# A streaming-encoder step: narrower gathered rows, a 112-sum top-k and gates from expert 68

## The chip, the cores and the metric

The kernel runs on one core of a Trainium2 chip. The metric is the device time of one execution in microseconds (us), lower is better. The engines are called as in the profile: PE (TensorE matmul), PEld (its weight loads), DVE (VectorE), ACT (ScalarE), POOL (GpSimd) and SP (SyncE, here only an issuer of DMAs).

## The reference, cut to what matters

One layer of an encoder over 288 tokens (256 of a prompt, 32 of a running stream), width 2048, in float32. First comes an attention mixer with an output projection and a layer norm, and then a mixer in which each token chooses among 16384 single-neuron experts. Only the second one is touched:

```python
q = (xt @ w_q).reshape(T, 8, 2, 128)
s = einsum('thcd,hcnd->thcn', q, sub_keys)              # 8 heads, 2 halves, 128 keys
sv, si = top_k(s, 16)
cand = sv[:, :, 0, :, None] + sv[:, :, 1, None, :]       # 16 x 16 sums per head
best, pos = top_k(cand, 16)
experts = si[.., pos // 16] * 128 + si[.., pos % 16]     # written with take_along_axis
gates = softmax(best)
out = sum over the 128 chosen experts of gelu(x . u[e]) * gate * v[e]
```

`sv` comes sorted from the largest down, so of the 256 sums of a head only those can be among the best 16 that have few enough sums above and to the left of them.

## The kernel before, in words

The work has five stages, one after the other on the PE: the projections and the attention; the output projection; the query projection of the experts (16 tiles, `proj(rh, rl, NQ)`); the **U stage**, which multiplies all 128 x 128 experts' u-rows with 224 of the tokens; and the **V stage**, which multiplies the gated activations with the v-rows. Every weight is split by ACT into a high part (L164) and by DVE into a rest (L180), and the PE multiplies both; in the U stage an expert block, called an expert from here on, takes 16 pairs of products (L976, L978).

The tokens are dealt with in three groups, `ROWS = (128, 96, 128)`: groups 0 and 1 are the 224 dense tokens. The last 64 tokens, the **gathered** ones (group 2), don't go through U and V: their u- and v-rows are fetched by indirect DMAs from POOL (`Rows.fetch`, L885) and multiplied on DVE (`use_u` L900, `use_v` L1063). Each of the 64 tokens stands twice, on partitions 0 to 63 with four heads and on 64 to 127 with the other four. So their normalised rows `x1g` are wanted on all 128 partitions.

`residual(c, ps)` (L605) runs once for each of the 16 column tiles of the output projection. It adds the residual, and on the PE it transposes two groups of 128 tokens (L614) and lays the 64 gathered tokens twice with two matmuls against the identity, one to each half of the partitions (L616). DVE then takes statistics (L619), and ACT copies the gathered part into `x1g` (L620). `norm_job` (L765) turns the statistics into mean and scale, and `rows_job` (L753) normalises `x1g` in two halves of 1024 columns (L757, L759, L761).

The work beside the products is interleaved by hand. `tick()` (L210) is called four times in each expert (after products 3 and 7 of each of its halves). A tick advances every generator in `stages` by a step, and then spends a budget on the queue `slow`: each tick adds `pace["rate"]` to it, and each `yield` of a generator in `slow` names the cost that is taken from it. The rate is 0.4 in the query stage (L861), 0.62 at the start of the U stage (L967), and `URATE = 0.38` from the moment that the gathered tokens' choice is known (L1015). In `slow` stand, in this order of completion: `rows_job`; `topk` for the pieces (0: heads 0, 4), (2: pairs 0-1), (2: pairs 2-3); `gathered_choice` (L741), which sets the flag for the rate; three more `topk` of group 0; `dense_choice(0)`; four `topk` of group 1; `dense_choice(1)`. A `topk` (L645) works on two heads at once: it finds the best 16 of 128 keys twice, forms the 256 sums (L677), finds the best 16 of them (L684 to L695), and recovers the two key numbers by a comparison with `iota`, a product and a sum (L702 to L709). A `dense_choice` (L727) makes the softmax on ACT and DVE, transposes the two key numbers and the gate on the PE (L733), copies them (L735) and negates the gate (L738).

From expert `G0` on, the gates of the dense tokens are made: one-hot matrices on DVE and ACT (`one_hots`, L903 to L912), two tokens for each half of an expert, four small matmuls on the PE (L956), and a product or copy into the activations (`gate_in`, L915). They take 112 halves, with four more for the pipeline. All of `slow` has to be done by then, so in expert `G0 - 1`, after its first half, the kernel empties the queue there and then, in program order:

```python
if i == G0 - 1 and half == 0:        # L996
    while slow:
        drain(slow.popleft())
...
if i < G0:                           # L1016
    ug.upto(GFIRST * (n + 1 - g_from) // (2 * G0 - g_from))
else:
    ug.upto(GFIRST + (128 - GFIRST) * (n + 1 - 2 * G0) // (2 * (NKEY - G0) - 4))
```

`ug.upto` paces the 128 gathered u-rows: `GFIRST = 40` of them before expert `G0`, and 88 after it. The order of the DMAs is that of POOL's program for the indirect ones and of SP's for the weights (L190).

Of the kernel before, what the change touches and what calls it, by code (L numbers as in the profile page):

```python
# [9 lines left out]
F32 = mybir.dt.float32  # L10
# [3 lines left out]
AF = mybir.ActivationFunctionType  # L14
OP = mybir.AluOpType
AX = mybir.AxisListType

P = 128
D = 2048
DT = 16  # L20
NTOK = 288
NQ = NTOK + 2
ND = 224
# [11 lines left out]
K = 16  # L35
# [5 lines left out]
KT = [0, 1, 2, 3, 4, 5, 6, 7, 8, 9, 12, 13, 14, 15, 10, 11]  # L41
AHEAD = 2
RAW = 4
G0 = 64
GFIRST = 40
VEND = 230
URATE = 0.38
# [3 lines left out]
def tile_stream_step(ctx: ExitStack, tc, xT_d, memT_d, ckT_d, cv_d, cmkT_d, cmv_d,  # L51
# [3 lines left out]
    nc = tc.nc  # L55
    const = ctx.enter_context(tc.tile_pool(name="const", bufs=1))
# [24 lines left out]
    x1g = keep.tile([P, D], F32, tag="x1g", name="x1g")  # L81
# [64 lines left out]
    at = {"load": 0, "split": 0, "take": 0}  # L146
# [108 lines left out]
    def rsqrt(pool, out, v, n, rows=P):  # L255
# [14 lines left out]
    ident = const.tile([P, P], F32, tag="ident", name="ident")  # L270
# [4 lines left out]
    iota = const.tile([P, NKEY], F32, tag="iota", name="iota")  # L275
    nc.gpsimd.iota(iota, pattern=[[1, NKEY]], base=0, channel_multiplier=0,
                   allow_small_or_imprecise_dtypes=True)
    lncol = const.tile([P, 2, DT], F32, tag="lncol", name="lncol")
    nc.gpsimd.dma_start(lncol, lncol_d)
    hot = memp.tile([32, NREL], F32, tag="hot", name="hot")  # L280
# [29 lines left out]
    for u in range(8):  # L310
        hi, lo = take()
# [282 lines left out]
    grow = nat.tile([P, 2, D], F32, tag="grow", name="grow")  # L594
    stat = nat.tile([P, 3, DT, 6], F32, tag="stat", name="stat")
    mvr = nat.tile([P, 3, 4], F32, tag="mvr", name="mvr")
    for c in range(0, DT, 4):
        nc.gpsimd.dma_start(rT[:, c:c + 4], xT_d[:, c:c + 4])

# [5 lines left out]
    def residual(c, ps):  # L605

        r, g = rT[:, c], lncol[:, 0, c:c + 1]
        nc.vector.scalar_tensor_tensor(r, r, ALPHA, ps[:, :NTOK], op0=OP.mult, op1=OP.add)
        nc.scalar.activation(rh[:, c, :NTOK], r, AF.Copy, scale=g)
        yield  # L610
        nc.vector.scalar_tensor_tensor(rl[:, c, :NTOK], r, g, rh[:, c, :NTOK].bitcast(F32), op0=OP.mult, op1=OP.subtract)
        tp = pb()
        for t in range(2):
            nc.tensor.transpose(tp[:, t * P:(t + 1) * P], r[:, t * P:(t + 1) * P], ident)  # L614
        for t in range(2):
            nc.tensor.matmul(tp[64 * t:64 * t + 64, 2 * P:3 * P], r[:, ND:NTOK], ident, start=True, stop=True)  # L616
        yield
        for t in range(3):
            nc.vector.bn_stats(stat[:, t, c], tp[:, t * P:(t + 1) * P])  # L619
        nc.scalar.copy(x1g[:, c * P:(c + 1) * P], tp[:, 2 * P:3 * P])  # L620

    def start_residual(c, ps):
        g = residual(c, ps)
# [21 lines left out]
    def topk(units):  # L645


        V = nc.vector
        n, t, R = len(units), units[0][0], ROWS[units[0][0]]
        key = f"{t}_{units[0][1]}"  # L650
        step = units[-1][1] - units[0][1] or 1
        hs = slice(units[0][1], units[-1][1] + 1, step)

        def new(tag, shape, dt=F32):
            return tw.tile([P, 2] + shape, dt, tag=tag, name=f"{tag}{key}")[:R, :n]
        S = [s_all[:R, u] for *_, u in units]
        sv, si, sf = new("sv", [2, K]), new("si", [2, K], U32), new("sf", [2, K])
        s2, ca, pos = new("s2", [2, NKEY]), new("ca", [K, K]), new("pos", [K], U32)
        ab, abf = new("ab", [2, K], U32), new("abf", [2, K])
        bv = best[:R, t, hs]  # L660
        both = [(q, c) for c in range(2) for q in range(n)]
        for q, c in both:
            V.max(out=sv[:, q, c, 0:8], in_=S[q][:, c])
        for q, c in both:
            V.max_index(out=si[:, q, c, 0:8], in_max=sv[:, q, c, 0:8], in_values=S[q][:, c])
            if c == 0 and q == n - 1:
                yield 0.64 * n
        yield 0.22 * n
        for q, c in both:
            V.match_replace(out=s2[:, q, c], in_to_replace=sv[:, q, c, 0:8], in_values=S[q][:, c], imm_value=-3.0e38)  # L670
        yield 0.43 * n
        for q, c in both:
            V.max(out=sv[:, q, c, 8:16], in_=s2[:, q, c])
        yield 0.43 * n
        for q, c in both:
            V.max_index(out=si[:, q, c, 8:16], in_max=sv[:, q, c, 8:16], in_values=s2[:, q, c])
        V.tensor_tensor(out=ca, in0=sv[:, :, 0].unsqueeze(3).to_broadcast([R, n, K, K]),  # L677
                        in1=sv[:, :, 1].unsqueeze(2).to_broadcast([R, n, K, K]), op=OP.add)
        yield 0.7 * n
        V.tensor_copy(sf.rearrange("p q c k -> p (q c k)"), si.rearrange("p q c k -> p (q c k)"))  # L680
        cf = [ca[:, q].rearrange("p a b -> p (a b)") for q in range(n)]
        c2 = [s2[:, q].rearrange("p a b -> p (a b)") for q in range(n)]
        for q in range(n):
            V.max(out=bv[:, q, 0:8], in_=cf[q])  # L684
        yield 0.4 * n
        for q in range(n):
            V.match_replace(out=c2[q], in_to_replace=bv[:, q, 0:8], in_values=cf[q], imm_value=-3.0e38)
        for q in range(n):
            V.max_index(out=pos[:, q, 0:8], in_max=bv[:, q, 0:8], in_values=cf[q])
        yield 0.7 * n  # L690
        for q in range(n):
            V.max(out=bv[:, q, 8:16], in_=c2[q])
        yield 0.35 * n
        for q in range(n):
            V.max_index(out=pos[:, q, 8:16], in_max=bv[:, q, 8:16], in_values=c2[q])  # L695
        V.tensor_scalar(ab[:, :, 0], pos, 4, None, op0=OP.logical_shift_right)
        V.tensor_scalar(ab[:, :, 1], pos, 15, None, op0=OP.bitwise_and)
        V.tensor_copy(abf.rearrange("p q c k -> p (q c k)"), ab.rearrange("p q c k -> p (q c k)"))
        yield 0.5 * n
        eq = (ca, s2.rearrange("p q c (a b) -> p q (c a) b", b=K))  # L700
        for c in range(2):
            V.tensor_tensor(out=eq[c], in0=iota[:R, 0:K].unsqueeze(1).unsqueeze(1).to_broadcast([R, n, K, K]),  # L702
                            in1=abf[:, :, c].unsqueeze(3).to_broadcast([R, n, K, K]), op=OP.is_equal)
        yield 0.62 * n
        for c in range(2):
            V.tensor_tensor(out=eq[c], in0=eq[c], in1=sf[:, :, c].unsqueeze(2).to_broadcast([R, n, K, K]), op=OP.mult)
        yield 0.62 * n
        for c, en in ((0, e1n), (1, e2n)):
            V.tensor_reduce(out=en[:R, t, hs], in_=eq[c], op=OP.add, axis=AX.X)  # L709
        yield 0.62 * n  # L710
# [41 lines left out]

    def rows_job():  # L753

        for a in range(2):
            cs = slice(a * 1024, (a + 1) * 1024)
            nc.scalar.activation(x1g[:, cs], x1g[:, cs], AF.Identity, bias=mvr[:, 2, 3:4], scale=mvr[:, 2, 2:3])  # L757
            yield 0.6
            nc.vector.tensor_mul(x1g[:, cs], x1g[:, cs], grow[:, 0, cs])  # L759
            yield 1.15  # L760
            nc.vector.tensor_add(x1g[:, cs], x1g[:, cs], grow[:, 1, cs])  # L761
            yield 1.15
        ns.close()

    def norm_job():  # L765

        yield
        for t in range(3):
            nc.vector.bn_aggr(mvr[:, t, 0:2], stat[:, t].rearrange("p a b -> p (a b)"))
        rsqrt(nat, mvr[:, :, 2], mvr[:, :, 1], 3)  # L770
        nc.vector.scalar_tensor_tensor(mvr[:, :, 3], mvr[:, :, 0], -1.0, mvr[:, :, 2], op0=OP.mult, op1=OP.mult)
        nc.vector.tensor_scalar(mvr[:, :, 0], mvr[:, :, 0], -1.0, None, op0=OP.mult)
        wide = nat.tile([P, 3, 2, P], F32, tag="wide", name="wide")
        for j in range(2):
            nc.vector.tensor_copy(wide[:, :, j], mvr[:, :, 2 * j:2 * j + 1].to_broadcast([P, 3, P]))
        yield
        yield
        yield
        tp = [pb(), pb()]
        for j in range(2):  # L780
            for t in range(2):
                nc.tensor.matmul(tp[j][:, t * P:(t + 1) * P], wide[:, t, j], ident, start=True, stop=True)
            nc.tensor.matmul(tp[j][:, 2 * P:NTOK], wide[32:64, 2, j], ident[32:64, 32:64], start=True, stop=True)
        yield
        for j in range(2):
            nc.scalar.copy(across[:, j], tp[j][:, :NTOK])
        flags["norm"] = True
        slow.append(rows_job())
        yield
        for d in range(DT):  # L790
            stages.append(normed(d))
            for _ in range(3 + d % 2):
                yield
# [174 lines left out]
    for i in range(NKEY):  # L968
        ps = pa()
        for half in range(2):  # L970
            n = 2 * i + half
            hi, lo = take()
# [8 lines left out]
            if n == 1:  # L981
# [5 lines left out]
                for h in range(0, 8, 2):  # L987
# [6 lines left out]
                                                                                 name="bigA")  # L994
# [348 lines left out]
```

## Time and profile before

| | |
|---|---|
| median of 3 runs | 2029.88 us (2026.51 to 2029.91) |
| the profiled execution | 2030.04 us, its span 2028.3 us |
| PE busy | 1988.4 us, 98% of the span |
| DVE busy | 1583.5 us, 78% |
| ACT busy | 1160.4 us, 57% |
| POOL busy | 496.7 us, 24% |

The span runs from the first to the last instruction, and the time holds some 1.7 us around it. A busy engine is one with an instruction under way. Matmuls overlap, so the duration of one is no measure of what it costs the PE; the distance between the starts of two is.

### The profile page before, as it was taken

How to read it: one execution, taken by the hardware profiler on the slowest of the kernel's cores; microseconds unless marked ns; L12 is line 12 of the kernel's file. 1: busy time of each engine (PE TensorE's matmuls, PEld its weight loads, DVE VectorE, ACT ScalarE, POOL GpSimd, SP SyncE). 2: the span in 40 equal slices, each digit the busy share in tenths (PEclk: the TensorE clock that was granted, in tenths of full speed). 3: DMA queues.
4: the chain of work that ended last, by engine and by line, in shares of the span. 5: the costliest groups of instructions: out<-in, count | busy, mean ns of one | idle time of the engine just before them, and what ended most of it. 6: DMA issues, size and time to landing. Idle time of an engine off the chain costs nothing.

```text
span 2028.3 us, 34887 instructions
## 1 busy us (share of the span) xinstructions
PE 1988.4 (98%) x13156; PEld 1871.1 (92%) x13156; DVE 1583.5 (78%) x2646; ACT 1160.4 (57%) x1916; POOL 496.7 (24%) x360
## 2 busy tenths in 40 slices
PE   9999999999999999998899999999999999999996
PEld 7999999999999999997899999999999999999996
DVE  5455555565789898899899999978888888888886
ACT  5445545533555555554799999954444445444453
POOL 0100000010000212122233333333444443343412
PEclk8999999999999999999899999999999999999998
DMA  7854455475456788887688888888999998999985
GB/s 269 267 165 149 147 158 150 128 250 148 147 155 187 265 280 278 275 276 258 216 295 296 296 294 302 295 305 302 335 328 340 327 328 318 327 324 328 324 264 170
DMA packets 145770, 520.43 MB, mean 257 GB/s; under 512 B 16785, under 2 KB 18977, under 8 KB 145473
## 3 DMA queue, kind: packets, MB, share of 16 engines
q1 hardware_dynamic: 101200, 358.66, 54.2%
q0 software_dynamic: 44400, 159.53, 21.5%
q8 instruction: 104, 1.70, 0.3%
q14 instruction: 66, 0.53, 0.1%
HBM read 507.54 MB, written 10.06 MB: 255 GB/s over the span
## 4 chain that ended last, share of the span: by engine, by line
PE 91%; DVE 5%; ACT 2%; DMA 1%; issue 1%; POOL 0%; SPq 0%; POOLq 0%; DVEq 0%; ACTq 0%
PE pa L976 21%; PE pa L1152 11%; PE pb L1152 11%; PE pa L978 10%; PE pa L231 7%; PE pa L232 6%; PE pa L233 6%; PE pb L1154 5%; PE pa L1154 5%; PE pb L956 2%; DVE lo L180 2%; ACT hi L164 1%; PE pa L931 1%; DMA raw<-in_wmv 1%; PE pb L396 0%
## 5 line engine op out<-in xcount | busy, mean ns | idle before, releaser
L180 DVE TENSOR_TENSOR lo<-raw,hi 128x1024 fp32r<-128x1024 f32 (+1 forms) x680 | 821.6, 1210 | 338.6 <-ACT hi L164 326.2
L164 ACT CAST hi<-raw 128x1024 fp32r<-128x1024 f32 (+1 forms) x680 | 705.8, 1039 | 448.0 <-PE pa L1152 277.2
L976 PE MATMUL pa<-ux,hi 128*128 128x448 f32 x2048 | 671.7, 379 | 0.0
L978 PE MATMUL pa<-ux,lo 128*128 128x224 f32 x2048 | 544.3, 266 | 0.9 <-DVE lo L180 0.9
L976 PEld LDWEIGHTS pa<-ux,hi 128*128 128x128 f32 x2048 | 386.4, 189 | 29.8 <-issue 0.2
L978 PEld LDWEIGHTS pa<-ux,lo 128*128 128x128 f32 x2048 | 392.4, 192 | 1.4 <-DVE lo L180 1.4
L1152 PE MATMUL pa<-hs,hi 128*128 128x448 f32 x1020 | 338.2, 376 | 0.0
L1152 PE MATMUL pb<-hs,hi 128*128 128x448 f32 x1020 | 337.9, 375 | 0.0
L885 POOL DMA_INDIRECT ur<-in_u,gidx x128 | 204.4, 1597 | 513.5 <-DVE ur L900 351.9
L885 POOL DMA_INDIRECT vr<-in_v,gidx x128 | 225.9, 1765 | 350.3 <-DVE x1g L1063 320.3
L1154 PE MATMUL pb<-hs,lo 128*128 128x224 f32 x1020 | 271.0, 266 | 0.3 <-DVE lo L180 0.3
L1154 PE MATMUL pa<-hs,lo 128*128 128x224 f32 x1020 | 270.9, 266 | 0.0
L1152 PEld LDWEIGHTS pb<-hs,hi 128*128 128x128 f32 x1020 | 191.4, 188 | 17.5
L1152 PEld LDWEIGHTS pa<-hs,hi 128*128 128x128 f32 x1020 | 191.4, 188 | 17.4
L1154 PEld LDWEIGHTS pb<-hs,lo 128*128 128x128 f32 x1020 | 194.8, 191 | 0.5 <-DVE lo L180 0.5
L231 PE MATMUL pa<-xh,hi 128*128 128x288 f32 x640 | 195.1, 305 | 0.0
L1154 PEld LDWEIGHTS pa<-hs,lo 128*128 128x128 f32 x1020 | 194.8, 191 | 0.0
L232 PE MATMUL pa<-xl,hi 128*128 128x288 f32 x640 | 188.8, 295 | 0.0
L233 PE MATMUL pa<-xh,lo 128*128 128x288 f32 x640 | 188.1, 294 | 0.0
L1063 DVE SCALAR_TENSOR_TENSOR x1g<-vr,ggate,x1g 128x1024 f32<-128x1024 f32 x128 | 163.6, 1278 | 0.0
L900 DVE SCALAR_TENSOR_TENSOR ur<-ur,x1g 128x1024 f32<-128x1024 f32 x128 | 155.7, 1216 | 2.3 <-DMA ur<-in_u,gidx 2.3
L231 PEld LDWEIGHTS pa<-xh,hi 128*128 128x128 f32 x640 | 120.0, 187 | 4.9 <-issue 3.7
(341 smaller groups left out, 2721.0 us busy)
## 6 DMA issues: line engine op xcount, KB each, us to landing
raw<-in_ut SPq DMA_DIRECT2D x256, 512.0 KB
raw<-in_v SPq DMA_DIRECT2D x255, 512.0 KB
raw<-in_win SPq DMA_DIRECT2D x80, 512.0 KB
raw<-in_wq SPq DMA_DIRECT2D x32, 512.0 KB
raw<-in_wo SPq DMA_DIRECT2D x29, 512.0 KB
raw<-in_wmv SPq DMA_DIRECT2D x8, 512.0 KB
raw<-in_wmk SPq DMA_DIRECT2D x6, 512.0 KB
rT<-in_xT POOLq DMA_DIRECT2D x4, 576.0 KB
```

Source lines behind the costliest of these rows:

```text
L164: nc.scalar.copy(hi[:, cs], raw[:, cs])
L180: nc.vector.tensor_sub(lo, raw, hi.bitcast(F32))
L231: nc.tensor.matmul(ps[:, :n], wh, mh[:, d, :n], start=(d == 0), stop=False)
L232: nc.tensor.matmul(ps[:, :n], wh, ml[:, d, :n], start=False, stop=False)
L233: nc.tensor.matmul(ps[:, :n], wl, mh[:, d, :n], start=False, stop=(d == DT - 1))
L885: nc.gpsimd.indirect_dma_start(out=t, out_offset=None, in_=self.table, in_offset=bass.IndirectOffsetOnAxis(ap=gidx[:, a, s:s + 1], axis=0))
L900: nc.vector.scalar_tensor_tensor(rows, rows, 1.0, x1g[:, a * 1024:(a + 1) * 1024], op0=OP.mult, op1=OP.mult, accum_out=gact[:, a, s:s + 1])
L976: nc.tensor.matmul(ps[:, :2 * ND], wh, ux[:, d].rearrange("p a t -> p (a t)"), start=(d == 0), stop=False, skip_group_check=True)
L978: nc.tensor.matmul(ps[:, :ND], wl, ux[:, d, 0], start=False, stop=False, skip_group_check=True)
L1063: nc.vector.scalar_tensor_tensor(va, rows, ggate[:, s:s + 1], va, op0=OP.mult, op1=OP.add)
L1152: nc.tensor.matmul(accs[dt][:, :2 * ND], wh, hb.rearrange("p a t -> p (a t)"), start=(i == 0), stop=False, skip_group_check=True)
L1154: nc.tensor.matmul(accs[dt][:, :ND], wl, hb[:, 0], start=False, stop=False, skip_group_check=True)
```

## The change

It has three parts. In `residual` one transpose lays the 64 gathered tokens on partitions 0 to 63 alone; the statistics, the copy and `rows_job` work on 64 partitions; and `rows_job` copies each half of the finished `x1g` to partitions 64 to 127 by a DMA from POOL. In `topk` the sums are 112 for each head, rows 0 to 3 of the first list with all 16 of the second, and rows 4 to 15 with the first 4 of the second; the position is turned back into two key numbers by comparisons with a new constant `first`; and the costs named at the `yield`s are lower. And `G0` is 68.

```diff
-G0 = 64
+G0 = 68
...
+    first = const.tile([P, 2, K], F32, tag="first", name="first")
+    nc.vector.tensor_scalar(first[:, 0], iota[:, 0:K], 16.0, None, op0=OP.mult)
+    nc.vector.tensor_scalar(first[:, 1], iota[:, 0:K], 4.0, 48.0, op0=OP.mult, op1=OP.add)
+    nc.vector.tensor_tensor(out=first[:, 0], in0=first[:, 0], in1=first[:, 1], op=OP.min)
...
+    nc.vector.memset(mvr[64:, 2], 1.0)
...
-        for t in range(2):
-            nc.tensor.matmul(tp[64 * t:64 * t + 64, 2 * P:3 * P], r[:, ND:NTOK], ident, start=True, stop=True)
-        yield
-        for t in range(3):
-            nc.vector.bn_stats(stat[:, t, c], tp[:, t * P:(t + 1) * P])
-        nc.scalar.copy(x1g[:, c * P:(c + 1) * P], tp[:, 2 * P:3 * P])
+        nc.tensor.transpose(tp[:64, 2 * P:3 * P], r[:, ND:NTOK], ident)
+        yield
+        for t, R in enumerate((P, P, 64)):
+            nc.vector.bn_stats(stat[:R, t, c], tp[:R, t * P:(t + 1) * P])
+        nc.scalar.copy(x1g[:64, c * P:(c + 1) * P], tp[:64, 2 * P:3 * P])
...
-        V.tensor_tensor(out=ca, in0=sv[:, :, 0].unsqueeze(3).to_broadcast([R, n, K, K]),
-                        in1=sv[:, :, 1].unsqueeze(2).to_broadcast([R, n, K, K]), op=OP.add)
-        yield 0.7 * n
+        cc = ca.rearrange("p q a b -> p q (a b)")
+        for lo, hi, m in ((0, 4, K), (4, K, 4)):
+            at = min(lo, 4) * K
+            V.tensor_tensor(out=cc[:, :, at:at + (hi - lo) * m].rearrange("p q (a b) -> p q a b", b=m),
+                            in0=sv[:, :, 0, lo:hi].unsqueeze(3).to_broadcast([R, n, hi - lo, m]),
+                            in1=sv[:, :, 1, 0:m].unsqueeze(2).to_broadcast([R, n, hi - lo, m]), op=OP.add)
+        yield 0.55 * n
         V.tensor_copy(sf.rearrange("p q c k -> p (q c k)"), si.rearrange("p q c k -> p (q c k)"))
-        cf = [ca[:, q].rearrange("p a b -> p (a b)") for q in range(n)]
-        c2 = [s2[:, q].rearrange("p a b -> p (a b)") for q in range(n)]
+        V.tensor_tensor(out=sf[:, :, 0, 1:], in0=sf[:, :, 0, 1:], in1=si[:, :, 0, :K - 1], op=OP.subtract)
+        cf = [cc[:, q, 0:112] for q in range(n)]
+        c2 = [s2[:, q].rearrange("p a b -> p (a b)")[:, 0:112] for q in range(n)]
...
-        yield 0.4 * n
+        yield 0.3 * n
...
-        yield 0.7 * n
+        yield 0.42 * n
...
-        yield 0.35 * n
...
-        V.tensor_scalar(ab[:, :, 0], pos, 4, None, op0=OP.logical_shift_right)
+        V.tensor_scalar(ab[:, :, 0], pos, 12, None, op0=OP.bitwise_and)
         V.tensor_scalar(ab[:, :, 1], pos, 15, None, op0=OP.bitwise_and)
-        V.tensor_copy(abf.rearrange("p q c k -> p (q c k)"), ab.rearrange("p q c k -> p (q c k)"))
-        yield 0.5 * n
+        V.tensor_copy(abf[:, :, 0], pos)
+        V.scalar_tensor_tensor(abf[:, :, 1], abf[:, :, 0], 64.0, ab[:, :, 0], op0=OP.is_ge, op1=OP.mult)
+        V.tensor_tensor(out=abf[:, :, 1], in0=ab[:, :, 1], in1=abf[:, :, 1], op=OP.subtract)
+        yield 0.65 * n
...
+        x = x1g[:64]
...
+            nc.gpsimd.dma_start(x1g[64:, cs], x1g[:64, cs])
```

The three instructions of `rows_job` and the third `bn_aggr` work on 64 partitions accordingly, and the comparison at L702 takes `first` with "greater or equal" for the first list and `iota` with "equal" for the second.

## Rows read from the trace of the kernel before

**Rows 1.** Page, parts 1 and 2: busy time per engine; granted TensorE clock in 40 slices

```profile
PE 1988.4 (98%) x13156; PEld 1871.1 (92%) x13156; DVE 1583.5 (78%) x2646; ACT 1160.4 (57%) x1916; POOL 496.7 (24%) x360
...
PEclk8999999999999999999899999999999999999998
```

**Rows 2.** Windows: us, then PE, PEld, DVE, ACT, POOL busy, clock, DMA share, GB/s

```profile
700.00:950.00 250.00, 250.00 (x1602) 237.49 (x1601) 224.39 (x479) 134.07 (x201) 57.43 (x35) 1.00 0.83 278
...
955.00:960.00 5.00, 0.00 (x0) 0.00 (x0) 5.00 (x34) 0.20 (x1) 1.14 (x1) 0.73 0.73 245
...
970.00:975.00 5.00, 4.70 (x18) 4.41 (x19) 2.83 (x5) 1.18 (x2) 0.38 (x1) 0.57 0.18 34
...
1000.00:1300.00 300.00, 300.00 (x2031) 286.88 (x2031) 275.84 (x538) 281.94 (x645) 109.95 (x71) 1.00 0.86 297
```

**Rows 3.** Waits of the PE, longest first: total us, times, longest

```profile
PE pb L733 <- DVE e1n L709: 13.3, 1, 13.3
```

**Rows 4.** Timeline of PE, 954 to 983 us: start, us, instruction, idle before

```profile
954.51 0.27 PE L978 MATMUL pa<-ux,lo 128*128 128x224 f32 x1
...
970.43 0.72 PE L976 MATMUL pa<-ux,hi 128*128 128x448 f32 x1
...
974.51 0.38 PE L976 MATMUL pa<-ux,hi 128*128 128x448 f32 x1
...
974.83 0.37 PE L976 MATMUL pa<-ux,hi 128*128 128x448 f32 x1
...
982.50 0.37 PE L931 MATMUL pa<-small,identr 128*128 128x224 f32 x1 [0.64 <-ACT small L929]
```

**Rows 5.** Timeline of DVE over the same stop, first and last piece of the selection

```profile
955.25 0.86 DVE L663 MAX8 sv<-s_all 96x8 f32<-96x128 f32 x4
...
967.96 0.67 DVE L709 TENSOR_REDUCE e2n<-s 96x32 f32<-96x512 f32 x1
```

**Rows 6.** Timeline of PE at 812 us: the first transpose of `dense_choice(0)`

```profile
812.37 0.27 PE L733 MATMUL pb<-ident,e1n 128*128 128x128 f32 x1
```

**Rows 7.** Groups by line and shape, DVE: count, busy us, mean ns

```profile
L676 DVE FIND_INDEX8 si<-sv,s 128x8 uint32<-128x128 f32 x24 | 6.4, 285 | 0.0
...
L695 DVE FIND_INDEX8 pos<-best,s 128x8 uint32<-128x256 f32 x12 | 4.9, 419 | 0.0
```

**Rows 8.** Timelines of PE and its weight loads around one residual, 503 to 505 us

```profile
503.35 0.38 PE L614 MATMUL pb<-ident,rT 128*128 128x128 f32 x2
...
503.66 0.44 PE L616 MATMUL pb<-ident,rT 128*64 128x128 f32 x4
...
504.26 0.30 PE L232 MATMUL pa<-rl,hi 128*128 128x290 f32 x1
...
504.40 0.30 PE L233 MATMUL pa<-rh,lo 128*128 128x290 f32 x1
...
503.65 0.20 PEld L616 LDWEIGHTS pb<-ident,rT 128*64 128x64 f32 x4 [0.17 <-issue]
...
504.02 0.19 PEld L231 LDWEIGHTS pa<-rh,hi 128*128 128x128 f32 x1 [0.17 <-issue]
```

**Rows 9.** Timeline of PE around transposes of 128 and 32 rows, 105 to 107 us

```profile
105.33 0.60 PE L380 MATMUL pb<-ident,vT 128*128 128x128 f32 x4
...
105.77 0.38 PE L382 MATMUL pb<-ident,vT 128*32 128x128 f32 x2
...
106.12 0.30 PE L232 MATMUL pa<-xl,hi 128*128 128x288 f32 x1
```

**Rows 10.** Groups of two lines: count, ns min/median/max, first and last start

```profile
L761 DVE TENSOR_TENSOR x1g<-x1g,grow x2: 1216/1218/1219, 519.3 to 533.5; 128x1024 f32<-128x1024 f32 x2
...
L885 POOL DMA_INDIRECT ur<-in_u,gidx x128: 936/1679/2880, 675.4 to 1337.3; - x128
```

**Rows 11.** Timeline of DVE at the start, 0 to 14 us

```profile
8.72 0.22 DVE L274 CAST identr<-ident 128x128 fp32r<-128x128 f32 x1
...
8.86 0.54 DVE L286 COPY relb<-rel 32x768 f32<-32x768 f32 x1
```

More of the change, by code (lines that the diff above doesn't have):

```diff
@@ L689, in topk @@
             V.max_index(out=pos[:, q, 0:8], in_max=bv[:, q, 0:8], in_values=cf[q])
-        yield 0.7 * n
+        yield 0.42 * n
         for q in range(n):
             V.max(out=bv[:, q, 8:16], in_=c2[q])
-        yield 0.35 * n
         for q in range(n):
             V.max_index(out=pos[:, q, 8:16], in_max=bv[:, q, 8:16], in_values=c2[q])
-        V.tensor_scalar(ab[:, :, 0], pos, 4, None, op0=OP.logical_shift_right)
+        V.tensor_scalar(ab[:, :, 0], pos, 12, None, op0=OP.bitwise_and)
         V.tensor_scalar(ab[:, :, 1], pos, 15, None, op0=OP.bitwise_and)
-        V.tensor_copy(abf.rearrange("p q c k -> p (q c k)"), ab.rearrange("p q c k -> p (q c k)"))
-        yield 0.5 * n
+        V.tensor_copy(abf[:, :, 0], pos)
+        V.scalar_tensor_tensor(abf[:, :, 1], abf[:, :, 0], 64.0, ab[:, :, 0], op0=OP.is_ge, op1=OP.mult)
+        V.tensor_tensor(out=abf[:, :, 1], in0=ab[:, :, 1], in1=abf[:, :, 1], op=OP.subtract)
+        yield 0.65 * n
         eq = (ca, s2.rearrange("p q c (a b) -> p q (c a) b", b=K))
         for c in range(2):
-            V.tensor_tensor(out=eq[c], in0=iota[:R, 0:K].unsqueeze(1).unsqueeze(1).to_broadcast([R, n, K, K]),
-                            in1=abf[:, :, c].unsqueeze(3).to_broadcast([R, n, K, K]), op=OP.is_equal)
+            V.tensor_tensor(out=eq[c], in0=abf[:, :, c].unsqueeze(3).to_broadcast([R, n, K, K]),
+                            in1=(first[:R, 0] if c == 0 else iota[:R, 0:K]).unsqueeze(1).unsqueeze(1).to_broadcast([R, n, K, K]),
+                            op=OP.is_ge if c == 0 else OP.is_equal)
         yield 0.62 * n
@@ L753, in rows_job @@
     def rows_job():
+        x = x1g[:64]
         for a in range(2):
             cs = slice(a * 1024, (a + 1) * 1024)
-            nc.scalar.activation(x1g[:, cs], x1g[:, cs], AF.Identity, bias=mvr[:, 2, 3:4], scale=mvr[:, 2, 2:3])
+            nc.scalar.activation(x[:, cs], x[:, cs], AF.Identity, bias=mvr[:64, 2, 3:4], scale=mvr[:64, 2, 2:3])
             yield 0.6
-            nc.vector.tensor_mul(x1g[:, cs], x1g[:, cs], grow[:, 0, cs])
+            nc.vector.tensor_mul(x[:, cs], x[:, cs], grow[:64, 0, cs])
             yield 1.15
-            nc.vector.tensor_add(x1g[:, cs], x1g[:, cs], grow[:, 1, cs])
+            nc.vector.tensor_add(x[:, cs], x[:, cs], grow[:64, 1, cs])
             yield 1.15
+            nc.gpsimd.dma_start(x1g[64:, cs], x1g[:64, cs])
         ns.close()
@@ L767, in norm_job @@
         yield
-        for t in range(3):
-            nc.vector.bn_aggr(mvr[:, t, 0:2], stat[:, t].rearrange("p a b -> p (a b)"))
+        for t, R in enumerate((P, P, 64)):
+            nc.vector.bn_aggr(mvr[:R, t, 0:2], stat[:R, t].rearrange("p a b -> p (a b)"))
         rsqrt(nat, mvr[:, :, 2], mvr[:, :, 1], 3)
```

## The prediction

> **What bounds the kernel now.** I read the page's busy times first. PE is busy for 1988.4 of 2028.3 us [rows 1], so 40 us of the span can be won by taking idle time from the PE; anything more has to come from PE work that is no longer done. The other engines matter only where the PE waits for them. The granted clock shows where to look: outside the first and the last slice it is below full in one slice alone, the twentieth, around 950 to 1000 us [rows 1]. The waits of the PE name the reason, 13.3 us in one piece at a transpose of `dense_choice` (L733), waiting for DVE's L709 [rows 3]. In the windows the PE does nothing from 955 to 960 us while DVE is busy for all 5.00 us, and afterwards it runs at a mean clock of 0.57; before and behind the stop it is busy for 250.00 of 250 and 300.00 of 300 us [rows 2]. So the rest of the U stage is PE-bound, and this stop is the drain of `slow` in expert `G0 - 1` = 63.
>
> The timeline gives its price. The low product at 954.51 ends a pair, and the next pair would start 0.10 us later. A pair is 974.83 - 974.51 = 0.32 us when the clock is full. The next one starts at 970.43, and 974.51 starts the eighth [rows 4]. On pace that is 954.61 + 7 x 0.32 = 956.85, or 957.2 with three transposes of about 0.11 us (worked out below) that are needed anyway. So the PE is 17.3 us late there: about 15.5 from the stop and 1.8 from the slow clock behind it. A further 0.64 us goes at 982.50, where ACT is behind [rows 4]. Together **18.0 us**.
>
> **The pacing: does the drain become empty?** DVE starts a whole `topk` just after the stop begins (L663 at 955.25) and ends its last sum at 967.96 [rows 5]; then comes `dense_choice(1)`. The same follows from the code. The costs at the yields of a `topk` sum to 6.23 x 2 = 12.46 units, of a `dense_choice` to 3.0 + 6 x 0.8 + 0.3 = 8.1. After the gathered choice there remain seven `topk` and two `dense_choice`, 103.4 units. Counting ticks, the flag comes at the end of expert 8; from there to the middle of expert 63 are 54.6 experts of 4 x 0.38 = 1.52 units, 83.0. About 20.4 are left, and one `topk` and one `dense_choice` are 20.56. The trace agrees also on the way: by this count the first transpose of `dense_choice(0)` falls in expert 36, and it stands at 812.37 [rows 6], 188 us or 36 experts of 5.2 us behind the start of the stage.
>
> After the change a `topk` costs 5.5 x 2 = 11.0 units, so 7 x 11.0 + 16.2 = 93.2 remain behind the flag. Three lighter `topk` ahead of the flag bring it 1.5 to 2 experts forward, to the start of expert 7. From there to the middle of expert 67 are about 60.2 experts, 91.5 units. Tick by tick the drain is left with 1.1 units, the last two yields of `dense_choice(1)`: the copy of the gate (ACT) and its negation (DVE). No PE instruction is among them, and the first gate matmul comes two ticks later at the earliest. Both edits are needed: with `G0` still 64 the same count leaves 7.3 units, and with the old costs at 68 it leaves 13.5. So I take **-18.0 us**, with 0 as the other end.
>
> **The residuals.** One residual's six matmul groups take 504.26 - 503.35 = 0.91 us until the second ordinary matmul behind them; less one ordinary distance of 0.14 (504.40 - 504.26), they cost the PE 0.77 us. The four passes of L616 lie between two idle times of 0.17 us that wait for nothing the profile names [rows 8]. In the attention, four transposes of 128 and two of 32 columns cost 106.12 - 105.33 - 0.13 = 0.66 us, 0.11 each, with no such gap [rows 9]. The new code has three transposes, 0.33 us, and saves 0.44 x 16 = **-7.1 us**. The stage is PE-bound, so that goes to the end. The bounds: if both gaps stay, 0.77 - 0.33 - 0.34 = 0.10, which is 1.6 us in all; if the narrow transpose is half price, 8.0. I take the attention's row, since it is the same kind of instruction.
>
> The Trainium skill, TensorEngine Tiling (Array Packing), section Key Properties, says that a change of the tiling mode drains the TensorE, and its section Available Configurations lists 128x64 as a mode of its own. If the new 64-column transpose ran in that mode it would drain twice as L616 does, and the sum would be that of the first rival; the 32-column transposes of the attention show no drain.
>
> **What costs nothing, and under what cover.** The shorter scans: a search over 128 elements takes 285 ns, over 256 it takes 419 [rows 7], 1.05 ns an element, so 144 elements fewer save 0.15 us in each of ten scans of a `topk`, and the sums save a little, while four more small instructions of about 0.2 us give some back: about 1 us of 13, all on DVE beside a PE that never waits [rows 2]. DVE is 90% busy there; if the lighter budgets ran ahead of it, lo parts would come late, but the real work per unit rises only from 13.3/12.46 to about 12.1/11.0, 3%.
>
> The DMA to the upper partitions comes after the second L761, which starts at 533.5, and the first gathered row is fetched at 675.4 [rows 10]; 140 us cover it. On POOL the two issues stand ahead of the writes of `x1Ts`, which are read a stage later. The 1.0 written into `mvr` stands on DVE where it waits for the residual's input anyway.
>
> The constant `first` puts three small DVE instructions ahead of `relb`, which the PE waits for; DVE is late there already. The nearest row is a small cast, 0.22 us, and the next the copy of 0.54 [rows 11]. Between 0 and 0.7 us; I take **+0.3**.
>
> Gates in 60 experts, not 64: they need 116 halves, and there are 120. The 88 later u-rows now come in 116 halves in place of 124, 7% denser. They ran from 970 to 1337 us [rows 4, 10], so some 72 fall in the 300 us of the window; 5 more of 1.2 us, the duration of a like instruction [rows 10], take DVE from 275.8 to 282 [rows 2]. ACT's 281.9 doesn't change. Below 300 I count 0.
>
> **The sum.** 2030.04 - 18.0 - 7.1 + 0.3 = 2005.2 us for the profiled execution. The median of the runs lies 0.16 us under that execution, so **2005 us**.
>
> **The rivals.**
> (a) The narrow transpose keeps the gaps of 0.17 us on both sides. For it speaks the shape 128*64 in the rows of L616, against it the 32-column one. Then 16 x 0.34 = 5.4 us come back: 2010.6 us. Chance 9%.
> (b) The drain isn't empty, because the order of the pieces differs from my count, or the PE waits in the ticks for the late transposes. If all of `dense_choice(1)` were left, the time from 968.6, where DVE is done with the sums, to 970.4 shows 2 us and a little clock: about 2008. With part of a `topk` in addition, up to 2018. Chance 9%.
> (c) Slower: from expert 68 DVE becomes the bound, because the gates and the denser u-rows crowd it, and lo parts come late. It decides once DVE's work in 300 us exceeds 300. To end at 2034 us, 29 us must be lost in a stage of some 340, so the work would have to be 325, against the 282 that I count. Chance 3%.
> (d) Nothing to see: the order on DVE puts a wait of 25 us elsewhere, at the first gates for instance. No row shows one; 2030 us, 2%.
>
> **How the numbers follow.** The forecast has 75%, and 2% are left for less than its range. The range must hold (a) and the light end of (b), the price of `first`, and the 3.4 us over which the three runs spread: 2001 to 2012. A measurement of this kernel can tell about 0.2%, 4 us, from no change. Faster by more than that are the forecast, (a), (b) and the low rest: 95%; same is (d), 2%; slower is (c), 3%.
>
> **What would show it.** Right: no wait at L733 in the PE's waits, a full clock from 700 to 1300 us, and the first gate matmuls (L956) four experts later with no stop ahead of them; one instruction where L616 had four, with no idle before it; DVE about 94% busy and the PE full in the gate stage. Wrong: a wait of the PE on DVE or ACT between experts 64 and 72, idle of 0.17 us at the narrow transposes, or waits for L180 in the gate stage.

## The result, and the profile after

The changed kernel takes 1993.49 us in the median of 4 runs (1992.35 to 1996.58), the kernel before 2029.89 us in 4 runs beside it (2026.51 to 2031.3). The ratio is 0.9825, with a 95% interval of 0.9808 to 0.9842. Forecast were 2005 us and a range of 2001 to 2012: the direction is right, but the time lies 11.5 us below the forecast and below the range. The profiled execution took 1992.35 us, 37.7 less than that of before, and its span is 1990.5 us. The lines below say L991 and L993 for the U products, L746 and L748 for the transposes of `dense_choice` and their copies, L620 for the transpose of the gathered tokens.

First the page, busy times and granted clock, to be read against [rows 1]:

```profile
PE 1968.3 (99%) x13108; PEld 1867.5 (94%) x13108; DVE 1569.2 (79%) x2686; ACT 1159.8 (58%) x1916; POOL 486.6 (24%) x362
...
PEclk9999999999999999999999999999999999999998
```

PE's busy time fell by 20.1 us, more than the residuals (7.1) and the slow products behind the stop can give; that is the first sign of something that the prediction didn't hold. The dip in the twentieth slice is gone, and so is the 8 in the first.

The waits of the PE, the longest four, and the windows of [rows 2] with one more in the V stage:

```profile
PE pb L247 <- POOL ident masks.py:199: 1.4, 1, 1.4
PE pb L619 <- DMA rT<-in_xT: 1.0, 1, 1.0
PE pb L299 <- DVE relb L290: 0.8, 1, 0.8
PE pb L451 <- DVE w L436: 0.7, 1, 0.7
```

```profile
700.00:950.00 250.00, 250.00 (x1602) 238.37 (x1601) 219.79 (x523) 136.19 (x202) 46.33 (x32) 1.00 0.82 272
955.00:960.00 5.00, 5.00 (x34) 4.78 (x33) 3.30 (x4) 2.84 (x5) 0.66 (x1) 1.00 0.91 314
970.00:975.00 5.00, 5.00 (x36) 4.80 (x35) 4.63 (x7) 4.86 (x13) 1.78 (x1) 1.00 0.81 284
1000.00:1300.00 300.00, 300.00 (x2034) 288.09 (x2033) 280.61 (x548) 282.08 (x645) 119.81 (x75) 1.00 0.87 307
1500.00:1600.00 100.00, 100.00 (x641) 95.45 (x640) 85.58 (x73) 50.26 (x50) 42.52 (x26) 1.00 0.94 335
```

No wait of the transposes of `dense_choice` is left ([rows 3] had 13.3 us), the PE is full from 955 to 975 us, and the gate stage is full too. The last line has its counterpart in this window of the kernel before:

```profile
1500.00:1600.00 100.00, 100.00 (x634) 94.57 (x633) 84.38 (x72) 49.48 (x49) 41.73 (x26) 1.00 0.93 330
```

Both PEs are busy for all 100 us at the full clock, and yet one starts 641 products in that time and the other 634. The V stage, which no part of the change touches, runs 1% faster. To see where the time went, the spans are cut at the first product of each stage:

| us | before | after | difference |
|---|---|---|---|
| start, to the first product on `xh` | 65.3 | 61.0 | -4.3 |
| projections and attention | 312.7 | 312.7 | 0.0 |
| output projection with its residuals | 123.7 | 117.6 | -6.1 |
| query projection | 122.1 | 122.0 | -0.1 |
| U stage | 732.6 | 712.0 | -20.6 |
| V stage | 653.0 | 646.4 | -6.6 |
| behind the last product of V | 18.9 | 18.8 | -0.1 |

The sum that was forecast (25 us) stands in two of these lines, with 26.7. The other 10.9 us are the start and the V stage. The start is told from the windows of 12 to 20 us, before and after:

```profile
12.00:20.00 8.00, 8.00 (x25) 5.18 (x25) 3.16 (x4) 3.97 (x6) 0.00 (x0) 0.50 0.86 301
```

```profile
12.00:20.00 8.00, 8.00 (x48) 5.66 (x46) 5.47 (x5) 5.81 (x8) 0.00 (x0) 1.00 0.87 285
```

In the profiled execution of before the clock was at its lower level there (0.50 is 1.2 GHz), in that of after it was at 2.4 GHz. Over the fourteen profiles of this study the first product on `xh` starts anywhere from 61.0 to 67.9 us, and it goes with that clock: four profiles with 0.50 in this window have it at 65.0 to 67.9 us, one with 0.61 at 64.0, and the nine with 0.89 to 1.00 at 61.0 to 62.7. Kernels with and without `first` are in both groups. So these 4.3 us are scatter between executions as far as the profiles show, and the experiments below ask about the V stage.

### The profile page after: what moved, and what is told of

Read it like the earlier page. It is cut to its first block, busy times and chain, and to the rows that moved or that the text cites. A ratio compares the mean times of both kernels' runs of the same rounds, so it can differ in the third digit from the quotient of the medians.

```text
span 1990.5 us, 34816 instructions
## 1 busy us (share of the span) xinstructions
PE 1968.3 (99%) x13108; PEld 1867.5 (94%) x13108; DVE 1569.2 (79%) x2686; ACT 1159.8 (58%) x1916; POOL 486.6 (24%) x362
## 4 chain that ended last, share of the span: by engine, by line
PE 94%; DVE 3%; DMA 1%; ACT 1%; issue 0%; POOL 0%; SPq 0%; POOLq 0%; ACTq 0%; DVEq 0%
PE pa L991 22%; PE pa L1167 11%; PE pb L1167 11%; PE pa L993 11%; PE pa L231 7%; PE pa L232 7%; PE pa L233 7%; PE pb L1169 5%; PE pa L1169 5%; PE pb L971 3%; DVE lo L180 1%; PE pa L946 1%; DMA raw<-in_wmk 1%; ACT hi L164 1%; DMA raw<-in_wmv 1%
## 5 line engine op out<-in xcount | busy, mean ns | idle before, releaser
L180 DVE TENSOR_TENSOR lo<-raw,hi 128x1024 fp32r<-128x1024 f32 (+1 forms) x680 | 821.5, 1210 | 327.5 <-ACT hi L164 318.5
L991 PE MATMUL pa<-ux,hi 128*128 128x448 f32 x2048 | 669.6, 379 | 0.0
L993 PE MATMUL pa<-ux,lo 128*128 128x224 f32 x2048 | 544.6, 266 | 0.0
L991 PEld LDWEIGHTS pa<-ux,hi 128*128 128x128 f32 x2048 | 386.9, 189 | 27.3 <-issue 0.2
L993 PEld LDWEIGHTS pa<-ux,lo 128*128 128x128 f32 x2048 | 392.6, 192 | 0.0
L900 POOL DMA_INDIRECT ur<-in_u,gidx x128 | 198.2, 1549 | 500.9 <-DVE ur L915 321.8
L900 POOL DMA_INDIRECT vr<-in_v,gidx x128 | 220.8, 1725 | 349.5 <-DVE x1g L1078 329.8
```

Of the source, the lines that this page charges most:

```text
L180: nc.vector.tensor_sub(lo, raw, hi.bitcast(F32))
L900: nc.gpsimd.indirect_dma_start(out=t, out_offset=None, in_=self.table, in_offset=bass.IndirectOffsetOnAxis(ap=gidx[:, a, s:s + 1], axis=0))
L991: nc.tensor.matmul(ps[:, :2 * ND], wh, ux[:, d].rearrange("p a t -> p (a t)"), start=(d == 0), stop=False, skip_group_check=True)
L993: nc.tensor.matmul(ps[:, :ND], wl, ux[:, d, 0], start=False, stop=False, skip_group_check=True)
```

## The experiments

The 1% in V could come from what the change does there (it does nothing in program order), from chance, or from something that the change moves without naming it. The constant `first` takes 128 bytes of each partition ahead of the buffers of the weight stream, and so `raw`, `hi`, `lo` and all tiles behind them lie 128 bytes higher. The first four runs take the parts one by one; they shared one chip and its runs of the kernel before, and so did e5 to e8, and the last four, on chips of their own.

**e1_const: the constant alone.** The kernel before with these lines, whose result nothing else reads:

```diff
+    first = const.tile([P, 2, K], F32, tag="first", name="first")
+    nc.vector.tensor_scalar(first[:, 0], iota[:, 0:K], 16.0, None, op0=OP.mult)
+    nc.vector.tensor_scalar(first[:, 1], iota[:, 0:K], 4.0, 48.0, op0=OP.mult, op1=OP.add)
+    nc.vector.tensor_tensor(out=first[:, 0], in0=first[:, 0], in1=first[:, 1], op=OP.min)
```

> The kernel before with the constant `first` alone (a tile of 128 bytes on each partition, which shifts what is laid behind it, and its three instructions); nothing reads it. Theory A, placement: the V stage's faster step in the changed kernel (2.515 us for each 128 rows of v, against 2.542) comes from the shifted addresses; then this kernel shows 2.515 in the V stage and is 6 to 7 us faster than before, 2023 us. Theory B, the V step belongs to the execution or to the chip: the V step stays at 2.542 or varies from run to run without regard to the kernel, and the time is that of before within 1 us (2030). Theory C, the V step comes from the new x1g, or from the later gates: 2.542 here, 2030 us. The start (first product of the projections at 65.3 us before, 61.0 in the changed kernel) comes out at 61 if the three instructions make it, and anywhere if it is chance.

Measured: 2020.12 us (5 runs, 2018.44 to 2023.2) against 2028.95; ratio 0.9959 (0.9945 to 0.9973). The V stage takes 646.4 us, as after the change, and the window shows its 640 products:

```profile
1500.00:1600.00 100.00, 100.00 (x640) 95.44 (x640) 85.45 (x73) 50.25 (x51) 42.05 (x26) 1.00 0.93 336
```

So 6.6 us of the gain come with a tile that does no work. Most of the rest of the profiled execution's gain is in the start (62.3 us), which scatters.

**e2_resid: the residuals alone.** One transpose, 64 partitions, the DMA; `topk` and `G0` as before.

```diff
-        for t in range(2):
-            nc.tensor.matmul(tp[64 * t:64 * t + 64, 2 * P:3 * P], r[:, ND:NTOK], ident, start=True, stop=True)
+        nc.tensor.transpose(tp[:64, 2 * P:3 * P], r[:, ND:NTOK], ident)
...
+            nc.gpsimd.dma_start(x1g[64:, cs], x1g[:64, cs])
```

> The narrow transposes and the copy of x1g by DMA alone, with the old top-k and the gates from expert 64. All theories: the stage of the residuals takes 117.6 us in place of 123.7, the stop in expert 63 stays, 13.3 us at the transpose. Theory A: V step 2.542, time 2024. Theory B: 2024 with the V step anywhere. Theory C with x1g as the cause: V step 2.515, time 2017.

Measured: 2022.38 us (7 runs, 2019.69 to 2024.99), ratio 0.997 (0.9958 to 0.9981). The output projection takes 117.7 us in place of 123.7, so 6.0 us less; the U stage stays (732.5, with the stop of 13.3 us) and V stays too (654.3, of which 0.8 is a single wait for `lo` at 1980 us that the profile of before hasn't). The DMA shows in no wait of the PE.

**e3_topk: the 112 sums alone**, with the constant and `G0 = 64`.

```diff
-G0 = 68
+G0 = 64
...
+            nc.tensor.matmul(tp[64 * t:64 * t + 64, 2 * P:3 * P], r[:, ND:NTOK], ident, start=True, stop=True)
```

> The 112 sums with their constant alone, gates from expert 64. By the count of the ticks the drain is left with 7.3 units, all of them dense_choice(1): its softmax, transposes and copies, some 2 us as in the kernel before, so the stop shrinks from 15.5 us and its slow clock to 2 to 4 us: 14 to 16 us less in the U stage. If the stop's price were the change of stage itself (new tiles, first one-hot matrices, the table of ACT), 5 us or more would stay. Theory A: V step 2.515, time 2007 to 2009. Theories B and C: V step 2.542, time 2014 to 2016.

Measured: 2004.36 us (4 runs, 2002.59 to 2006.68), ratio 0.9879 (0.9863 to 0.9896). The U stage takes 714.6 us, 18.0 less than before. Of the waits of the PE in that stage one of the drain is left, for the last transpose:

```profile
PE pb L746 <- DVE best L737: 1.5, 1, 1.5
```

V takes 646.5 us, since the constant is in. 18.0 us here and 6.5 there are the whole gain.

**e4_g68: the later gates alone.** One line:

```diff
-G0 = 64
+G0 = 68
```

> The gates from expert 68 alone. By the count the drain is left with 13.5 units: the second half of a topk (from the maximum of the second eight on) and all of dense_choice(1); by the pieces of before 5.7 and 2 us. So the stop shrinks to about 8 us with some slow clock behind it, and the U stage is 8 to 10 us shorter. Theory A: V step 2.542, time 2020 to 2022. Theory C with the later gates as the cause: V step 2.515, time 2014. If the denser u-rows crowd DVE, the gate stage, 337.6 us from the first to the last of its matmuls, grows by more than 2 us.

Measured: 2020.17 us (4 runs, 2019.59 to 2021.26), ratio 0.9958 (0.9941 to 0.9974). The U stage takes 726.4 us, 6.2 less, which is under the expected 8 to 10. V stays at 653.1. The gates take 337.4 us from the first to the last matmul, 337.6 before, so nothing is crowded. The waits of the PE in the U stage:

```profile
PE pb L733 <- DVE e1n L709: 6.8, 1, 6.8
PE pb L733 <- DVE best L724: 1.2, 1, 1.2
```

Half of the waiting is still there (6.8 us of 13.3), but by estimate two thirds of the price: 18.0 - 6.2 = 11.8 us. Beside the waits the price holds the slow clock, which the windows behind this stop show for longer than the one behind the stop of before, where the clock was full again from 975 us on:

```profile
975.00:980.00 5.00, 0.42 (x1) 0.18 (x1) 4.90 (x15) 0.00 (x0) 0.00 (x0) 0.69 0.47 182
980.00:985.00 5.00, 3.69 (x13) 3.23 (x14) 2.99 (x9) 1.75 (x5) 0.00 (x0) 0.50 0.00 0
985.00:990.00 5.00, 5.00 (x27) 4.70 (x27) 2.35 (x4) 3.06 (x5) 0.94 (x1) 0.78 0.71 208
```

So a stop of half the length doesn't cost half. The count leaves 13.5 of 20.56 units in this kernel: all of `dense_choice(1)` (8.1) and 5.4 of a `topk`. The units aren't worth the same in time. Those of a `topk` are all DVE work, some 13 us for 12.46 units; those of a `dense_choice` hold the PE for 1 to 2 us together. So 5.4 units of `topk` keep a wait of 6.8 us, with the slow clock in addition, and in e3, whose 7.3 units all belong to `dense_choice`, a wait of 1.5 us is kept; the clock stays at 1.00 behind it.

**e5_keep: the whole change, the constant elsewhere.** `first` lies behind the stream's buffers, which are back in their old place.

```diff
-    first = const.tile([P, 2, K], F32, tag="first", name="first")
...
+    first = keep.tile([P, 2, K], F32, tag="first", name="first")
```

> The whole change, with `first` laid behind the tiles of `keep` and not in `const`, so that the stream's buffers (raw, hi, lo), x1g and the indices lie where they lay before the change, and only what stands behind `keep` is shifted by 128 bytes. If the place of the stream's buffers (or of x1g) sets the V step: 2.542 us, V stage 653 us and 1999 to 2001 us in all, 6.6 above the changed kernel. If the place of what lies behind (bigA, the gathered rows) sets it: 2.515 and 1993.

Measured: 2003.74 us (4 runs, 2001.34 to 2006.04), ratio 0.9883 (0.9867 to 0.99) to 2027.74 us for the kernel before, where the change as it stands has 0.9825 (0.9808 to 0.9842). V takes 653.0 us again, at the old 634 products:

```profile
1500.00:1600.00 100.00, 100.00 (x634) 94.47 (x633) 83.89 (x73) 50.23 (x50) 41.81 (x26) 1.00 0.94 336
```

The U stage keeps its gain (712.3 us). The time lies above the expected 1999 to 2001. Without the move the change gives 24 us, where the sum said 25. That this is so close is in part luck, since two terms are off in opposite directions: in this profile the U stage gives 20.3 us where 18.0 were forecast, and the output projection (118.3 us) 5.4 where 7.1 were.

**e6_pad64, e7_keep64, e8_keep32: other distances.** The changed kernel with 64 bytes more ahead of the stream, so 192 in all; and e5 with 64 and with 32 bytes ahead of it.

```diff
+    const.tile([P, 16], F32, tag="pad", name="pad")
```

This is the line of e6 and e7; e8 has `[P, 8]`.

> The changed kernel with 64 more unused bytes in `const`: the stream's buffers lie 192 bytes behind their old place, not 128. If the V step depends on the place in a pattern that 64 bytes change, it goes back to 2.54 (time 2000) or takes a third value; if any place but the old one is good, it stays at 2.515 (1993). The U step, 5.163 us an expert before its gates, was the same at both places; a change of it here would be new, and 1% of it is 3 us.

> The whole change with `first` behind `keep` and 64 unused bytes in its place in `const`: the stream's buffers lie 64 bytes behind their old place. A good place only at a step of 128 bytes gives 2.542 and 2000 us; any place but the old one, 2.515 and 1993 us.

> As the run with 64 bytes, with 32. The same two values by the same two theories; a value between 2.515 and 2.542 would say that the step depends on the place by degrees.

Measured, one run each: e6 1990.89 us, V 647.2; e7 1999.87 us, V 650.9; e8 2003.33 us, V 649.0. The windows of V, in turn e6, e7 and twice e8:

```profile
1500.00:1600.00 100.00, 100.00 (x641) 95.53 (x640) 85.38 (x74) 49.72 (x51) 42.27 (x26) 1.00 0.93 333
...
1500.00:1600.00 100.00, 100.00 (x636) 95.24 (x635) 83.94 (x73) 50.29 (x50) 42.40 (x26) 1.00 0.93 336
...
1500.00:1600.00 100.00, 100.00 (x635) 94.97 (x635) 84.15 (x72) 49.53 (x50) 43.54 (x26) 1.00 0.93 334
1700.00:1800.00 100.00, 100.00 (x640) 95.84 (x639) 84.95 (x73) 50.27 (x51) 40.33 (x23) 1.00 0.92 325
```

The time of V depends on the distance, but not in proportion to it, and neither of e7's two theories holds: its pace is a third one. In e8 the pace even changes within the stage, from 635 products to 640, so its V time of 649.0 us is a mixture. In all fourteen profiles the windows of 1500 to 1600, 1700 to 1800 and 1800 to 1900 us hold 633 or 634, 635 or 636, or 640 or 641 products, and no number between. The mean distance between the starts of two high products is 316.7, 315.6 or 313.3 ns at these paces.

**f1_hilo, f2_lo, f3_behind: which tile is it?** The kernel before with 128 free bytes at three places: behind `raw`, so that `hi`, `lo` and the rest move; between `hi` and `lo`; and behind `lo`, so that `x1g` and the rest alone move.

```diff
+            strm.tile([P, 32], F32, tag="pad", name="pad", bufs=1)
```

> The kernel before, with 128 bytes per partition left free between the raw buffers of the weight stream and its hi and lo buffers: the raw buffers stay in their place, hi, lo and all that lies behind them move by 128 bytes; the computation is untouched. Theory A (the V step of 2.515 us in place of 2.542 comes from where the PE's operands hi and lo lie): 2.515 us, V stage 646.4 us, span some 7 us under the kernel before, about 2021 to 2023 us. Theory B (it comes from where the raw buffers lie, into which the weights' DMAs write, or from the constants): 2.542 us, V stage 653, 2028 to 2030 us.

> The same with the 128 bytes between the hi and the lo buffers: only lo and what lies behind it moves. If the place of hi decides: V step 2.542 us, V stage 653, some 2029 us. If the place of lo (or its distance from hi) decides: 2.515 us, 646.4, some 2022 us. A value between the two would say that both buffers have a share.

> The same with the 128 bytes behind the stream's buffers, ahead of x1g and the gates' tiles: raw, hi and lo all stay. Theory A (operands of the PE): V step 2.542 us, V stage 653, some 2029 us. The rival (the rows x1g and the other tiles that DVE, ACT and POOL use, through what these engines do beside the PE): 2.515 us and some 2022 us.

Measured, one run each beside 2029.29 us of the kernel before (7 runs): f1 2019.95, f2 2017.87, f3 2025.31 us. V takes 647.0, 646.4 and 653.1 us. The windows of V, first f2:

```profile
1500.00:1600.00 100.00, 100.00 (x641) 95.38 (x640) 85.28 (x73) 49.92 (x50) 39.25 (x25) 1.00 0.93 333
```

and f3:

```profile
1500.00:1600.00 100.00, 100.00 (x634) 94.53 (x633) 84.57 (x72) 49.58 (x50) 41.90 (x26) 1.00 0.93 330
```

In f2 `raw` and `hi` lie where they lay before, and V is fast. In f3 all that lies behind `lo` is moved and `lo` isn't, and V is slow. So it is the place of `lo`; a move of 128 bytes is enough. Its distance from `hi` or `raw` isn't what counts, since in e1 and in the changed kernel all three move together and V is fast too. The rivals, `raw` as the DMAs' target and the rows that DVE uses, fall. f2's U stage is 2.4 us shorter too, f1's 0.8 and e1's 0.4, so that isn't a steady effect. f3's 2025.31 us lie below the kernel before, but its start took 61.0 us, as short as any here.

**f4_best: e6 again, timed.**

> The changed kernel with 64 more bytes per partition ahead of the stream's buffers, the kernel of the run e6_pad64 again, timed this time. If its expert step of 5.14 us in the U stage (5.16 in the changed kernel) belongs to the place, U takes 708 us again and the time is 1989 to 1992 us, some 2 to 3 us under the changed kernel. If it was chance, U takes 712 and the time 1992 to 1996 us.

Measured: 1995.52 us (4 runs, 1994.37 to 1997.12), ratio 0.9836 (0.982 to 0.9853). U takes 708.4 us again, so by two executions its 3.6 us belong to the place. But V takes 649.8 us, where the same program took 647.2 in e6:

```profile
1500.00:1600.00 100.00, 100.00 (x636) 94.91 (x635) 84.94 (x73) 50.32 (x50) 43.44 (x26) 1.00 0.94 334
```

The interval overlaps that of the changed kernel; no version here is shown to beat it. And at this distance the pace of V is not fixed by the program alone.

## Why the prediction was right or wrong

**The step that failed** is one that cost no sentence: the sum had no term for the V stage. The prediction found the PE full "before and behind the stop", took from that that only idle time or removed work could be won there, and costed `first` as three small DVE instructions and no more. A full PE isn't a PE at one pace. What `first` did beside its instructions was to move `lo`, and with it the V products went from 634 to 641 in 100 us. The five profiled kernels with `lo` 128 bytes higher (after, e1, e3, f1, f2) have 640 or 641 and a V stage of 646.4 to 647.0 us; the five with `lo` in its old place (before, e2, e4, e5, f3) have 634 and 653.0 to 654.3. As the pace is not always fixed by the place (f4, e8), it is this five against five, on several chips, and the runs of e5 and of the changed kernel, which don't overlap, that show the place as the cause at 128 bytes. With e5, where the place is the only thing taken back, the median is 2003.74 us, 1.3 below the forecast. e5 and the changed kernel lie 10.3 us apart by their medians and 9.0 by their profiled executions; of these 6.6 are V, 1.2 the start, 0.7 the residuals and 0.3 the U stage, and the last 0.2 are spread.

By the medians the miss is 11.5 us: 6.6 are V, and the U stage gave 2.6 more than was forecast and the residuals 1.0 less. Some 3 us are left, which the interval of the ratio covers (3.4 us either way) and which no run assigns to a part of the change.

Why `lo` at another place makes the products quicker is open. The PE waits for nothing of over 0.3 us there in these profiles, but for once 0.8 us in e2 and once 0.6 in f1; the distance of the products is 1% shorter throughout the stage. An obvious suspect is a collision with DVE's writes into `lo`, and the traces speak against it. From 1500 to 1900 us the mean distance between two high products is in the kernel before 316.4 ns where DVE writes `lo` over more than 90% of it (469 distances) and 316.4 where it writes none (472). In e5 both are 316.7, in f2 both 313.2, after the change 314.0 and 314.1. So the slower pace doesn't come and go with DVE's writes. What the PE's own reads have to do with it no run tells.

**The start** makes 4.3 us of the difference between the two profiled executions, but it isn't shown to be a part of the miss, as it scatters with either kernel. The range held 3.4 us for the scatter of runs; over all profiles this one stage scatters by 6.9 us.

**The drain: right, and a little more.** Forecast were -18.0 us. The waits of the PE in the U stage of before sum to 16.6 us (13.3, 1.2, 0.9, 0.6, 0.4, 0.2), and after the change the view lists none for that stage. Of the 20.6 us of the stage, 18.0 were forecast as the drain with its slow clock and the wait at 982.50. Another 1.3 are the two waits of 0.9 (L978 for L180, at 683 us, soon after the first gathered row is fetched) and 0.4 (L810 for the query's copy), for which the prediction had no term, since it put the lighter `topk` at nothing beside a PE that never waits. Neither wait is left in e3, which has the 112 sums alone, and e4 with the old `topk` still has both (0.7 and 0.4), so it is the lighter `topk` that removed them. In the view of before for this stage they stand as:

```profile
PE pa L978 <- DVE lo L180: 0.9, 1, 0.9
...
PE pb L810 <- ACT qT L841: 0.4, 1, 0.4
```

The last 1.3 us are not split; the gates, 337.6 us before and 336.3 after, hold as much. The pacing count was right as well. It left the last two yields of `dense_choice(1)`, and the timeline of after around it reads:

```profile
957.81 0.25 PE L746 MATMUL pb<-ident,e2n 96*128 96x96 f32 x1
...
963.07 0.25 PE L746 MATMUL pb<-ident,best 96*128 96x96 f32 x1
...
963.36 0.24 ACT L748 COPY gT<-pb 128x96 f32<-128x96 f32 x1 [0.98 <-PE pb L746]
963.63 0.21 DVE L751 TENSOR_SCALAR ngT<-gT 128x96 f32<-128x96 f32 x1 [0.44 <-ACT gT L748]
```

The copy and the negation follow the transpose at once, as a drain of 1.1 units would do it, and the PE goes on, so the rival of a drain that isn't empty falls. One sentence was wrong in its size: "with `G0` still 64 the same count leaves 7.3 units", from which it said that both edits are needed. e3 shows 18.0 of the 20.6 us without the second one, since those units are light on the PE. The scans came out as worked out: 419 ns at 256 elements [rows 7] became 270 at 112, 0.15 us less.

```profile
L704 DVE FIND_INDEX8 pos<-best,s 128x8 uint32<-128x112 f32 x12 | 3.1, 270 | 0.0
```

**The residuals: right in price, a little less in effect.** Around one residual the timeline of PE and weight loads is now, in answer to [rows 8]:

```profile
492.91 0.38 PE L619 MATMUL pb<-ident,rT 128*128 128x128 f32 x2
493.02 0.11 PEld L620 LDWEIGHTS pb<-ident,rT 128*64 128x64 f32 x1
493.13 0.27 PE L620 MATMUL pb<-ident,rT 128*64 128x128 f32 x1
...
493.38 0.29 PE L232 MATMUL pa<-rl,hi 128*128 128x290 f32 x1
...
493.51 0.30 PE L233 MATMUL pa<-rh,lo 128*128 128x290 f32 x1
```

493.38 - 492.91 less an ordinary distance of 0.13 is 0.34 us, where 0.33 were forecast, and no idle time stands before the weight load of L620. The stage gives 6.1 us, not 7.1 (6.0 in e2, 5.4 in e5). One of the sixteen residuals runs behind the first product of the query stage, so 15 x 0.44 = 6.6 fall here; and the weight loads now wait longer for DVE's residual, as their waits over this stage show, before and after:

```profile
PEld pa L231 <- issue: 2.8, 15, 0.4
PEld pb L616 <- issue: 2.5, 15, 0.2
PEld pb L614 <- DVE rT L608: 1.3, 1, 1.3
```

```profile
PEld pb L619 <- DVE rT L613: 2.0, 3, 1.3
...
PEld pa L231 <- issue: 0.4, 1, 0.4
```

The gaps on both sides are gone, and 0.7 us has come back as a wait for DVE. The first rival, that the narrow transposes keep their gaps, is thereby refuted. The Trainium skill, TensorEngine Tiling (Array Packing), Key Properties, which the prediction put beside it, says that a change of the tiling mode drains the TensorE. The trace doesn't show such a drain for L620, though its tile is 128*64 like that of L616, which had idle time on both sides. So the width of the tile alone doesn't make the gap. What does (the half of the columns that is written, the several passes, or that L616 was an ordinary product) was not tried.

**What was costed at nothing.** The gate stage: DVE is busy for 280.61 of 300 us, forecast 282, ACT for 282.08, forecast 281.9, and the PE is full. The slower rival needed DVE beyond 300 us and falls with that line. The DMA to the upper partitions shows in no wait. Of the 0.3 us for `first` at the start nothing is seen: the PE waits 0.8 us for `relb`, 1.2 before, though DVE starts it 0.45 us later (9.31 against 8.86 in [rows 11]).

```profile
8.94 0.17 DVE L279 TENSOR_SCALAR first<-iota 128x16 f32<-128x16 f32 x1
9.01 0.17 DVE L280 TENSOR_SCALAR first<-iota 128x16 f32<-128x16 f32 x1
9.21 0.17 DVE L281 TENSOR_TENSOR first<-first 128x16 f32<-128x16 f32 x1
9.31 0.54 DVE L290 COPY relb<-rel 32x768 f32<-32x768 f32 x1
```

The rival by which nothing would be seen falls too: no other wait took the place of the stop.

## What to carry to other kernels

A change that adds or resizes a tile also moves every tile behind it, and a stage in which the PE is never idle can change its pace by 1% from that alone; where a gain is larger than its terms, count the products in 100 us of a stage that the change doesn't touch, and run the change once more with the new tile at another place. A queue that is paced by estimated costs is judged by what the leftover units do on the engines, since units of equal size were worth a wait of 1.3 us each in one generator, with a slow clock behind it, and of 0.2 in the other. And the span of one profiled execution carries the scatter of its start, here up to 6.9 us; a difference between two profiles is read with that in mind.

## What the runs showed of the hardware

With the PE busy for 100.00 of 100 us at the full clock, the same products ran at 634 or 640 to 641 in 100 us, by the place of one of the stream's three kinds of buffers (old place or 128 bytes on, five profiles each); moves by 32, 64 and 192 bytes gave 635 to 636 or 640 to 641. The pace didn't differ between moments at which DVE wrote that buffer and moments at which it didn't (316.4 ns a pair in both, before). At 192 bytes the same program ran at 641 in one execution and at 636 in another, and at 32 bytes it changed from 635 to 640 within one. A wait of the PE of 13.3 us and one of 6.8 us were each followed by a stretch at the lower clock, one of 1.5 us (e3) was not. And a transpose into 64 columns went through behind two of 128 columns and ahead of an ordinary product with no idle time, 0.34 us for three, where ordinary products with weights of the same shape had 0.17 us of idle time on both sides.
